# A two-layer decoder trunk on one core: routing pieces and low parts in strict turns on VectorE, scores one head ahead, the table's first tile asked for earlier

## Chip, cores and metric

One core of one Trainium2 chip runs the whole program in one launch. The metric is the device time of one execution in microseconds; lower is better. Engines are called by the profile's names: PE (TensorE, matrix multiplication), DVE (VectorE), ACT (ScalarE), POOL (GpSimd) and SP (the engine whose queue issues most DMAs).

## What is computed

A decoder trunk of two layers on 256 tokens of width 1024, float32: a recurrent block, then a stick-breaking attention block. Each is followed by the same product-key expert layer, which is where the change lies:

```python
q = (xt @ w_q).reshape(T, PEER_HEADS, 2, PEER_HALF)
s = jnp.einsum('thpd,hpnd->thpn', q, sub_keys)
sv, si = lax.top_k(s, PEER_TOPK)
cand = sv[:, :, 0, :, None] + sv[:, :, 1, None, :]
cv, ci = lax.top_k(cand.reshape(T, PEER_HEADS, PEER_TOPK * PEER_TOPK), PEER_TOPK)
i1 = jnp.take_along_axis(si[:, :, 0], ci // PEER_TOPK, axis=-1)
i2 = jnp.take_along_axis(si[:, :, 1], ci % PEER_TOPK, axis=-1)
eidx = (i1 * PEER_NKEYS + i2).reshape(T, PEER_HEADS * PEER_TOPK)
gates = jax.nn.softmax(cv, axis=-1).reshape(T, PEER_HEADS * PEER_TOPK)
...
act = jax.nn.gelu(jnp.einsum('cd,ckd->ck', xc, u_tab[ic]))
return jnp.einsum('ck,ckd->cd', gc * act, v_tab[ic])
```

There are 8 heads, 128 keys per half, 16 picks per head, and 128 x 128 = 16384 experts with a row each in the tables `u` and `v`.

## The kernel before

**The up stage.** For 224 of the 256 tokens the kernel does not gather expert rows. It multiplies the whole table `u` with the tokens in 128 tiles (`e` = 0 to 127), 128 experts each, applies gelu, multiplies by a gate that is zero for experts not picked, and then multiplies with the 128 tiles of `v` (the v stage, tile name `acc`). The other 32 tokens take their rows by gathered DMAs (`fetches`, `fetch_row`; tiles `got`, `rows`, `sums`).

**Halves.** A float32 product is made of three matmuls. `split` makes, of a raw tile, a rounded high part on ACT (`wH`, the copy in `split`) and the rest, the low part, on DVE (`wL`, line 136). A tile of 128 x 1024 takes 24 matmuls in `mm3`, lines 165 to 167; of each three, line 167's needs `wL`, so the third matmul of a tile already waits for the low part. `fetch` asks for the raw tile on SP, from a pool of three buffers `raws`, and splits it into a pool of three pairs `halves`. A raw buffer is free once ACT and DVE have read it.

**Routing.** `route` is a generator, one per head. Its first step multiplies the tokens with the two `w_q` tiles of the head, copies the result (`qT`, ACT) and multiplies it with the keys into scores `ps_s`. Each later step is a piece of DVE work: four max pieces (16 largest of 128 keys, with indices, lines 497 to 501), two candidate pieces (lines 506 to 522), one that splits the index (527 to 540), one that makes a one-hot `hot` (543), one that multiplies it (551), and one that sums it to `picks`, `places` and `shares` (556 to 564). Heads 0 and 1 have their scores before the loop. From `e` = 4 on each tile of the up stage draws two steps from the generators, one head after the other. When they are used up, the tile number is kept as `begun`, which comes out as 47.

**What follows routing.** `scatter` writes a head's gates for 128 of the tokens into a table `G` in DRAM, by indirect DMAs on POOL; the other 96 tokens' gates are made by `hots` (DVE), eight matmuls and a product in `bank_of_gates`, in 24 groups spread over the tiles from `begun` to 124. From `e` = 52 on, every fourth tile (every second from 116) makes one step of `fetches`, and draws four scatters. In the v stage the gates in `G` come back in tiles `gt` of four experts' tiles each; `gates(0)` asks for the first after the up stage's loop, and line 792 multiplies with it.

**Order.** A scheduler places each engine's instructions. `issue_after(i)` holds what is traced in its block behind the instruction `i` if it is on the same engine; pieces are held behind the last low part traced so far, `self.lows[-1]`. Low parts are not held behind pieces. `load` holds its DMA behind the last raw tile's.

Of the kernel before, what the change touches and what calls it, by code (L numbers as in the profile page):

```python
# [8 lines left out]
F32 = mybir.dt.float32  # L9
# [10 lines left out]
P = 128  # L20
# [4 lines left out]
NK = 128  # L25
# [31 lines left out]
class Trunk:  # L57


    def __init__(self, ctx, tc, a):  # L60
# [11 lines left out]
        self.n = 0  # L72
        self.lows = []

        c = self.const
# [58 lines left out]
    def split(self, raw, hi, lo):  # L134
        self.copied = self.nc.scalar.copy(out=hi, in_=raw)  # L135
        self.lows.append(self.nc.vector.tensor_tensor(out=lo, in0=raw, in1=hi.bitcast(F32), op=ALU.subtract))  # L136
        return hi, lo

# [332 lines left out]
    def route(self, l, hd, pool, xs, r):  # L471
# [21 lines left out]
        for t in range(2):  # L493
            for p in range(2):
                yield
                s, s2 = S[:, t, p], tl([P, NK], F32, "s2")
                V.max(out=sv[:, t, p, :8], in_=s)
                V.match_replace(out=s2, in_to_replace=sv[:, t, p, :8], in_values=s, imm_value=LOWEST)  # L498
                V.max(out=sv[:, t, p, 8:], in_=s2)
                V.max_index(out=si[:, t, p, :8], in_max=sv[:, t, p, :8], in_values=s)  # L500
                V.max_index(out=si[:, t, p, 8:], in_max=sv[:, t, p, 8:], in_values=s2)
        yield
# [13 lines left out]
        for t in range(2):  # L516
            s = cand[:, t]
            V.max(out=cv[:, t, :8], in_=s)
            V.match_replace(out=cand2, in_to_replace=cv[:, t, :8], in_values=s, imm_value=LOWEST)
            V.max(out=cv[:, t, 8:], in_=cand2)  # L520
            V.max_index(out=ci[:, t * K:t * K + 8], in_max=cv[:, t, :8], in_values=s)
            V.max_index(out=ci[:, t * K + 8:(t + 1) * K], in_max=cv[:, t, 8:], in_values=cand2)
            if t == 0:
                yield
# [3 lines left out]
        if r is not None:  # L528
# [10 lines left out]
        V.tensor_tensor(out=ab[:, :, 1], in0=col, in1=tail, op=ALU.subtract)  # L539
        V.tensor_tensor(out=ab[:, :, 1], in0=ab[:, :, 1], in1=b8, op=ALU.add)  # L540
        yield
        hot = tl([P, 4 * K, K], BF16, "hot")
        V.tensor_tensor(out=hot, in0=self.iota.unsqueeze(1).to_broadcast([P, 4 * K, K]),
                        in1=ab.rearrange("p k x -> p (k x)").unsqueeze(2).to_broadcast([P, 4 * K, K]),
# [3 lines left out]
        with self.tc.issue_after(self.copied.ins):  # L548
            nc.scalar.activation(gt, gt, AF.Exp)
        h4 = hot.rearrange("p (t k x) a -> p t k (x a)", t=2, x=2)  # L550
        V.tensor_tensor(out=h4, in0=h4,
                        in1=sif.rearrange("p t x a -> p t (x a)").unsqueeze(2).to_broadcast([P, 2, K, 2 * K]),
# [10 lines left out]
        V.reciprocal(gs, gs)  # L563
        V.tensor_tensor(out=self.shares[:, :, ks], in0=gt, in1=gs.to_broadcast([P, 2, K]), op=ALU.mult)
        if hd < HEADS // 2:
            for _ in self.scatter(l, hd):
                pass
        if hd % (HEADS // 2) == HEADS // 2 - 1:
            self.name_rows(hd // (HEADS // 2))
        yield  # L570
# [116 lines left out]
    def peer(self, l):  # L687
# [3 lines left out]
        with ExitStack() as ph:  # L691
            ph.enter_context(self.early_pool)
            early = self.early
            with ExitStack() as up:
                pool = up.enter_context(tc.tile_pool(name="up", bufs=1, reuse_waits="tile"))
# [37 lines left out]
                heads += [self.route(l, hd, rt, xs, None) for hd in range(NX, HEADS)]  # L733
                pieces = (hd for hd in heads for _ in hd)
                made, done, begun = [], 0, None
                writes = (i for hd in range(HEADS // 2, HEADS) for i in self.scatter(l, hd))
                rows = self.fetches(l)
                for e in range(NK):
                    if begun is None and e >= 4:
                        for _ in range(2):  # L740
                            with tc.issue_after(self.lows[-1].ins):
                                if next(pieces, None) is None:
                                    begun = begun or e
# [7 lines left out]

                    if begun and e >= 52 and (e % 4 == 0 if e < 116 else e % 2 == 0):
                        with tc.issue_after(self.lows[-1].ins):
                            next(rows)
                        with tc.issue_after(self.row.ins):
                            for _ in range(4):
# [14 lines left out]
                    if done:  # L771
                        V.tensor_tensor(out=A[:, e, split:], in0=g, in1=A[:, e, split:], op=ALU.mult)
                assert done == NQ and next(writes, None) is None
            acc = [self.ps_acc.tile([P, 2, T], F32, tag=f"acc{i}", name=self.uid("acc")) for i in range(4)]
            proj_pool = side.enter_context(tc.tile_pool(name="proj", bufs=1, reuse_waits="tile"))
            late = ph.enter_context(tc.tile_pool(name="late", bufs=3, reuse_waits="tile"))

            def gates(e):
                pool = late if e else early
                gt = pool.tile([P, NB, TS], F32, tag="gt", name=self.uid("gt"))  # L780
                self.load(gt, self.G[l].rearrange("(p e t) one -> p e (t one)", p=NK, t=TS)[:, e:e + NB])
                return gt

            ahead, tail = gates(0), []
            self.sums = late.tile([P, D], F32, tag="sums", name=self.uid("sums"), bufs=1)
# [170 lines left out]
```

## Time and profile before

| | us |
|---|---|
| median of 3 runs | 1962.94 (1960.91 to 1966.56) |
| the profiled execution | 1962.31 |
| its span, first to last instruction | 1960.6 |
| PE busy | 1857.8 (95%) |
| DVE busy | 1524.5 (78%) |
| ACT busy | 1007.3 (51%) |
| POOL busy | 740.6 (38%) |

The mean granted PE clock is 0.982. A row of the timeline gives start and length in us, engine, line, operation, the tiles it writes and reads, and in brackets the idle time of the engine just before it and what ended it. A row of the waits gives who waited for whom, the total in us, how often, and the longest. Rows of `DMA` in the chain give the start, and the time from issue to landing as far as it lies on the chain. Line numbers are those of the kernel before; in the changed kernel they stand 1 to 20 lines further down.

### The profile page before, as it was taken

The page shows a single profiled execution, that of the slowest core. Times are in us where ns is not written, and L with a number is a line of the kernel's source. Part 1 is how long each engine was busy: PE and PEld are TensorE (multiplying, and loading weights), DVE is VectorE, ACT ScalarE, POOL GpSimd, SP SyncE. Part 2 cuts the span into 40 slices and gives each one's busy share as a digit, 9 for nine tenths or more (in the row PEclk, how much of TensorE's full clock was granted, in tenths as well). Part 3 has the DMA queues.
Part 4 walks back from the last instruction along what each step waited for, and adds up shares of the span by engine and source line. Part 5 has one row for each costly group of instructions (what it writes and reads, how often), then busy time and mean ns, then how long its engine had stood idle before and what let it go on. Part 6 is the DMA issues. An engine that isn't in the chain of part 4 may idle for free.

```text
span 1960.6 us, 40513 instructions
## 1 busy us (share of the span) xinstructions
PE 1857.8 (95%) x15716; PEld 1815.1 (93%) x15716; DVE 1524.5 (78%) x3255; ACT 1007.3 (51%) x1768; POOL 740.6 (38%) x517
## 2 busy tenths in 40 slices
PE   7898889999989999999999988889999999999998
PEld 6898889999989999998887988889999999999997
DVE  6888887878877877776755787877888877777766
ACT  6764444444435454445655644445444445454446
POOL 3318771777522112110200167744877221112102
PEclk9999999999999999999999999999999999999999
DMA  8756666788878888885681566657888788888863
GB/s 278 218 175 163 150 158 185 224 218 224 227 250 296 296 285 284 290 275 177 212 266 60 164 156 165 151 168 203 228 226 222 241 292 280 290 288 282 290 223 106
DMA packets 193394, 435.73 MB, mean 222 GB/s; under 512 B 51568, under 2 KB 87536, under 8 KB 193200
## 3 DMA queue, kind: packets, MB, share of 16 engines
q1 hardware_dynamic: 137104, 365.02, 57.4%
q0 software_dynamic: 56096, 68.12, 15.3%
q8 instruction: 123, 2.02, 0.4%
q14 instruction: 71, 0.58, 0.1%
HBM read 414.25 MB, written 17.96 MB: 220 GB/s over the span
## 4 chain that ended last, share of the span: by engine, by line
PE 70%; DVE 18%; DMA 4%; ACT 4%; issue 3%; SPq 0%; POOL 0%; DVEq 0%; ACTq 0%
PE acc L167 10%; PE acc L166 10%; PE acc L165 10%; DVE wL L136 6%; PE lin L167 6%; PE lin L165 6%; PE lin L166 6%; PE u L167 4%; PE u L165 4%; PE u L166 4%; ACT wH L135 2%; PE gates L673 2%; DMA raw<-v 2%; DMA gt<-G 1%; DVE s L498 1%
## 5 line engine op out<-in xcount | busy, mean ns | idle before, releaser
L136 DVE TENSOR_TENSOR wL<-raw,wH 128x1024 fp32r<-128x1024 f32 x620 | 758.1, 1224 | 323.2 <-ACT wH L135 305.0
L135 ACT CAST wH<-raw 128x1024 fp32r<-128x1024 f32 x620 | 649.5, 1049 | 658.1 <-PE acc L166 198.6
L165 PE MATMUL acc<-aH,wH 128*128 128x224 f32 x2048 | 565.7, 276 | 7.7 <-ACT wH L135 6.2
L167 PE MATMUL acc<-aH,wL 128*128 128x224 f32 x2048 | 567.5, 277 | 1.4 <-DVE wL L136 1.4
L166 PE MATMUL acc<-aL,wH 128*128 128x224 f32 x2048 | 564.0, 275 | 0.6 <-DVE aL L136 0.3
L578 POOL DMA_INDIRECT G<-shares,places x256 | 473.7, 1850 | 138.4 <-issue 80.7
L165 PEld LDWEIGHTS acc<-aH,wH 128*128 128x128 f32 x2048 | 395.8, 193 | 8.4 <-ACT wH L135 6.6
L167 PEld LDWEIGHTS acc<-aH,wL 128*128 128x128 f32 x2048 | 395.8, 193 | 1.8 <-DVE wL L136 1.8
L166 PEld LDWEIGHTS acc<-aL,wH 128*128 128x128 f32 x2048 | 395.8, 193 | 1.3 <-DVE aL L136 0.8
L603 POOL DMA_INDIRECT got<-v,named x64 | 90.0, 1407 | 418.1 <-DVE act L792 405.3
L603 POOL DMA_INDIRECT got<-rows,named x64 | 92.0, 1438 | 240.0 <-DVE got L620 160.0
L221 POOL TENSOR_TENSOR tot<-tot,sq 128x256 f32<-128x256 f32 x36 | 30.8, 855 | 264.5 <-ACT sq L219 263.3
L135 ACT CAST aH<-act 128x224 fp32r<-128x224 f32 x256 | 95.4, 375 | 14.1 <-DVE act L792 14.1
L136 DVE TENSOR_TENSOR aL<-act,aH 128x224 fp32r<-128x224 f32 x256 | 97.8, 383 | 0.9 <-ACT aH L135 0.9
L678 ACT COPY act<-gates 128x308 f32<-128x308 f32 (+23 forms) x48 | 14.0, 292 | 140.2 <-DVE act L677 131.6
L792 DVE TENSOR_TENSOR act<-act,gt 128x128 f32<-128x128 f32 x256 | 72.4, 283 | 11.3 <-DMA gt<-G 11.3
L659 DVE SCALAR_TENSOR_TENSOR first<-ints,which,gate 128x256 fp32r<-128x256 f32 x192 | 80.6, 477 | 0.0
L625 DVE SCALAR_TENSOR_TENSOR sums<-got,heat,sums 128x1024 f32<-128x1024 f32 x62 | 79.2, 1277 | 0.0
L620 DVE SCALAR_TENSOR_TENSOR got<-got,xrow 128x1024 f32<-128x1024 f32 x64 | 77.9, 1217 | 0.0
L167 PE MATMUL lin<-x0H,wL 128*128 128x224 f32 (+1 forms) x156 | 45.6, 292 | 25.8 <-DVE wL L136 25.8
L167 PEld LDWEIGHTS lin<-x0H,wL 128*128 128x128 f32 x156 | 30.3, 194 | 29.6 <-DVE wL L136 29.6
L167 PE MATMUL u<-x0H,wL 128*128 128x224 f32 x128 | 37.4, 292 | 19.2 <-DVE wL L136 19.1
(907 smaller groups left out, 5213.6 us busy)
## 6 DMA issues: line engine op xcount, KB each, us to landing
raw<-u SPq DMA_DIRECT2D x256, 512.0 KB
raw<-v SPq DMA_DIRECT2D x256, 512.0 KB
G<-zero SPq DMA_DIRECT2D x32, 512.0 KB
raw<-w_q SPq DMA_DIRECT2D x32, 512.0 KB
gt<-G SPq DMA_DIRECT2D x64, 256.0 KB
raw<-w_in SPq DMA_DIRECT2D x16, 512.0 KB
raw<-w_gate SPq DMA_DIRECT2D x16, 512.0 KB
raw<-w_out SPq DMA_DIRECT2D x8, 512.0 KB
```

The costliest lines, as they stand in the source:

```text
L135: self.copied = self.nc.scalar.copy(out=hi, in_=raw)
L136: self.lows.append(self.nc.vector.tensor_tensor(out=lo, in0=raw, in1=hi.bitcast(F32), op=ALU.subtract))
L165: mm(out, lhsT=sH, rhs=mH, start=start, stop=False, skip_group_check=True)
L166: mm(out, lhsT=sH, rhs=mL, start=False, stop=False, skip_group_check=True)
L167: self.product = mm(out, lhsT=sL, rhs=mH, start=False, stop=stop, skip_group_check=True)
L578: i = nc.gpsimd.indirect_dma_start(out=self.G[l][:, :], out_offset=bass.IndirectOffsetOnAxis(ap=self.places[:, k:k + 1], axis=0), in_=self ...
L603: self.row = self.nc.gpsimd.indirect_dma_start(out=got[:, :], out_offset=None, in_=table, in_offset=bass.IndirectOffsetOnAxis(ap=self.name ...
L620: V.scalar_tensor_tensor(out=row, in0=row, scalar=1.0, in1=self.xrow, op0=ALU.mult, op1=ALU.mult, accum_out=heat[:, i:i + 1])
L625: V.scalar_tensor_tensor(out=self.sums, in0=row, scalar=heat[:, i:i + 1], in1=self.sums, op0=ALU.mult, op1=ALU.add)
L659: V.scalar_tensor_tensor(out=first[:, j], in0=self.ints.unsqueeze(1).to_broadcast([P, 2, NK]), scalar=self.which[:, 0, t:t + 1], in1=self. ...
L673: nc.tensor.matmul(ps[:, j], lhsT=second[:, j], rhs=first[:, j, x], start=j == 0 and x == 0, stop=x == 1, skip_group_check=True)
L792: V.tensor_tensor(out=A[:, e, :TS], in0=A[:, e, :TS], in1=gt[:, e % NB], op=ALU.mult)
```

## The change

Three things change in each of the two expert layers.

1. `route` keeps the last DVE instruction of each piece as `self.mark`, and the next low part that `split` makes is held behind it. The tiles from `e` = 4 draw one step (even `e`) or two (odd `e`) instead of two. A head's first step, with the scores, is no longer a step of its own: it is made when the fourth max piece of the head before is reached. So 80 steps are drawn instead of 86, and `begun` comes out as 57.
2. The steps of `fetches` at `e` = 52 and 56 no longer wait for `begun`. The second `name_rows`, which makes the row numbers of heads 4 to 7, moves from the last piece of head 7 to `e` = 72.
3. `gates(0)` moves from behind the up stage's loop to the end of its tile 123.

```diff
     def split(self, raw, hi, lo):
         self.copied = self.nc.scalar.copy(out=hi, in_=raw)
         self.lows.append(self.nc.vector.tensor_tensor(out=lo, in0=raw, in1=hi.bitcast(F32), op=ALU.subtract))
+        if self.mark is not None:
+            self.after(self.lows[-1], self.mark)
+            self.mark = None
         return hi, lo
...
-                V.max_index(out=si[:, t, p, 8:], in_max=sv[:, t, p, 8:], in_values=s2)
+                self.mark = V.max_index(out=si[:, t, p, 8:], in_max=sv[:, t, p, 8:], in_values=s2)
...
-        if hd % (HEADS // 2) == HEADS // 2 - 1:
-            self.name_rows(hd // (HEADS // 2))
+        if hd == HEADS // 2 - 1:
+            self.name_rows(0)
...
-                pieces = (hd for hd in heads for _ in hd)
-                made, done, begun = [], 0, None
+
+                def in_turn():
+
+                    for i, hd in enumerate(heads):
+                        for n, _ in enumerate(hd):
+                            if n == 3 and NX <= i + 1 < HEADS:
+                                next(heads[i + 1])
+                            yield
+                pieces = in_turn()
+                made, done, begun, ahead = [], 0, None, None
...
                     if begun is None and e >= 4:
-                        for _ in range(2):
+                        for _ in range(1 + e % 2):
                             with tc.issue_after(self.lows[-1].ins):
-                                if next(pieces, None) is None:
+                                if next(pieces, pieces) is pieces:
                                     begun = begun or e
...
-                    if begun and e >= 52 and (e % 4 == 0 if e < 116 else e % 2 == 0):
+                    if e >= 52 and (e % 4 == 0 if e < 116 else e % 2 == 0):
                         with tc.issue_after(self.lows[-1].ins):
                             next(rows)
+                        if e == 72:
+                            with tc.issue_after(self.lows[-1].ins):
+                                self.name_rows(1)
...
-                assert done == NQ and next(writes, None) is None
+                    if e == NK - 5:
+                        assert next(writes, None) is None
+                        ahead = gates(0)
+                assert done == NQ
...
-            ahead, tail = gates(0), []
+            tail = []
```

The same `self.mark =` stands before the last DVE instruction of every other piece of `route`. `gates` itself is moved ahead of the stage, unchanged.

On DVE, in routing of layer 0 (`wL` are low parts; `sv`, `si` and `s` are one head's values, indices and masked scores). Before, the two low parts are followed by the head's max pieces, and the next low part stands only after 42 routing instructions:

```order
L136 TENSOR_TENSOR wL_2347<-raw_2344,wH_2346 128x1024
L136 TENSOR_TENSOR wL_2398<-raw_2395,wH_2397 128x1024
L497 MAX sv_2291<-ps_s_2220 128x8
L498 MATCH_REPLACE s_371_2293<-sv_2291,ps_s_2220 128x128
L500 MAX_INDEX si_2292<-sv_2291,ps_s_2220 128x8
L499 MAX sv_2291<-s_371_2293 128x8
L497 MAX sv_2291<-ps_s_2220 128x8
L501 MAX_INDEX si_2292<-sv_2291,s_371_2293 128x8
```

In the changed kernel, at the same head:

```order
L137 TENSOR_TENSOR wL_2398<-raw_2395,wH_2397 128x1024
L501 MAX sv_2196<-ps_s_2125 128x8
L502 MATCH_REPLACE s_388_2427<-sv_2196,ps_s_2125 128x128
L504 MAX_INDEX si_2197<-sv_2196,ps_s_2125 128x8
L503 MAX sv_2196<-s_388_2427 128x8
L505 MAX_INDEX si_2197<-sv_2196,s_388_2427 128x8
L137 TENSOR_TENSOR wL_2437<-raw_2434,wH_2436 128x1024
L501 MAX sv_2196<-ps_s_2125 128x8
```

A low part now stands behind each piece or two, and the five instructions of a single piece follow each other with nothing of another piece between them.

On SP, at the end of layer 0's up stage (`raw<-u` and `raw<-v` are table tiles, `gt<-G` the gate tiles), before:

```order
L158 DMA raw_7523<-u 128x1024
L158 DMA raw_7561<-u 128x1024
L148 DMA gt_7607<-G_145 128x512
L158 DMA raw_7617<-v 128x1024
L158 DMA raw_7655<-v 128x1024
```

and in the changed kernel:

```order
L162 DMA raw_7359<-u 128x1024
L152 DMA gt_7404<-G_145 128x512
L162 DMA raw_7406<-u 128x1024
L162 DMA raw_7451<-u 128x1024
L162 DMA raw_7498<-u 128x1024
L162 DMA raw_7536<-u 128x1024
L162 DMA raw_7590<-v 128x1024
```

The first gate tile moves ahead of four loads of `u`. The second keeps its place, behind the sixth load of `v`.

More of the change, by code (lines that the diff above doesn't have):

```diff
@@ L136, in split @@
         self.lows.append(self.nc.vector.tensor_tensor(out=lo, in0=raw, in1=hi.bitcast(F32), op=ALU.subtract))
+        if self.mark is not None:
+            self.after(self.lows[-1], self.mark)
+            self.mark = None
         return hi, lo
@@ L521, in route @@
             V.max_index(out=ci[:, t * K:t * K + 8], in_max=cv[:, t, :8], in_values=s)
-            V.max_index(out=ci[:, t * K + 8:(t + 1) * K], in_max=cv[:, t, 8:], in_values=cand2)
+            self.mark = V.max_index(out=ci[:, t * K + 8:(t + 1) * K], in_max=cv[:, t, 8:], in_values=cand2)
             if t == 0:
@@ L539, in route @@
         V.tensor_tensor(out=ab[:, :, 1], in0=col, in1=tail, op=ALU.subtract)
-        V.tensor_tensor(out=ab[:, :, 1], in0=ab[:, :, 1], in1=b8, op=ALU.add)
+        self.mark = V.tensor_tensor(out=ab[:, :, 1], in0=ab[:, :, 1], in1=b8, op=ALU.add)
         yield
         hot = tl([P, 4 * K, K], BF16, "hot")
-        V.tensor_tensor(out=hot, in0=self.iota.unsqueeze(1).to_broadcast([P, 4 * K, K]),
+        self.mark = V.tensor_tensor(out=hot, in0=self.iota.unsqueeze(1).to_broadcast([P, 4 * K, K]),
                         in1=ab.rearrange("p k x -> p (k x)").unsqueeze(2).to_broadcast([P, 4 * K, K]),
@@ L550, in route @@
         h4 = hot.rearrange("p (t k x) a -> p t k (x a)", t=2, x=2)
-        V.tensor_tensor(out=h4, in0=h4,
+        self.mark = V.tensor_tensor(out=h4, in0=h4,
                         in1=sif.rearrange("p t x a -> p t (x a)").unsqueeze(2).to_broadcast([P, 2, K, 2 * K]),
@@ L563, in route @@
         V.reciprocal(gs, gs)
-        V.tensor_tensor(out=self.shares[:, :, ks], in0=gt, in1=gs.to_broadcast([P, 2, K]), op=ALU.mult)
+        self.mark = V.tensor_tensor(out=self.shares[:, :, ks], in0=gt, in1=gs.to_broadcast([P, 2, K]), op=ALU.mult)
         if hd < HEADS // 2:
@@ L693, in peer, with gates @@
             early = self.early
+            def gates(e):
+                pool = late if e else early
+                gt = pool.tile([P, NB, TS], F32, tag="gt", name=self.uid("gt"))
+                self.load(gt, self.G[l].rearrange("(p e t) one -> p e (t one)", p=NK, t=TS)[:, e:e + NB])
+                return gt
             with ExitStack() as up:
@@ L776, in peer @@
             late = ph.enter_context(tc.tile_pool(name="late", bufs=3, reuse_waits="tile"))
[L778 to L782, printed above, removed]
-            ahead, tail = gates(0), []
+            tail = []
             self.sums = late.tile([P, D], F32, tag="sums", name=self.uid("sums"), bufs=1)
```

## The prediction

> **What bounds the kernel now.** I read the page first: engine shares, and the chain of work that ended last.
>
> ```profile
> PE 1857.8 (95%) x15716; PEld 1815.1 (93%) x15716; DVE 1524.5 (78%) x3255; ACT 1007.3 (51%) x1768; POOL 740.6 (38%) x517
> PE 70%; DVE 18%; DMA 4%; ACT 4%; issue 3%; SPq 0%; POOL 0%; DVEq 0%; ACTq 0%
> ```
>
> TensorE (PE) is the bound, but VectorE (DVE) carries 18% of the chain. To see where, I asked for busy time by stretch: layer 0 and layer 1 from the first matmul of tile e=4 to that of tile e=47, where routing ends, and then a stretch of the same loop without routing.
>
> ```profile
> 131.08:325.10 194.02, 169.28 (x1377) 164.68 (x1375) 162.00 (x590) 93.83 (x134) 128.05 (x78) 0.96 0.63 160
> 1125.66:1320.88 195.22, 169.12 (x1377) 164.20 (x1375) 162.24 (x590) 93.83 (x134) 129.70 (x78) 0.96 0.63 159
> 340.00:560.00 220.00, 219.85 (x1969) 219.67 (x1969) 180.22 (x324) 104.77 (x246) 142.79 (x80) 1.00 0.81 224
> ```
>
> The columns are length, then busy us and instructions of PE, weight loads, DVE, ACT, POOL, then granted clock, DMA share, GB/s. Without routing PE is busy all the time. With routing it is idle for 24.7 us of 194 and its clock averages 0.96. What PE waits for in layer 0's stretch:
>
> ```profile
> PE lin L167 <- DVE wL L136: 12.7, 10, 2.8
> PE u L167 <- DVE wL L136: 8.5, 8, 2.6
> PE ps_s L489 <- ACT qT L487: 3.1, 6, 0.5
> ```
>
> 21.2 of the 24.7 us is a late low part (wL). The DVE timeline of one head says why, and PE's shows the effect:
>
> ```profile
> 224.64 1.23 DVE L136 TENSOR_TENSOR wL<-raw,wH 128x1024 fp32r<-128x1024 f32 x1 [0.99 <-ACT wH L135]
> 225.78 0.29 DVE L497 MAX8 sv<-ps_s 128x8 f32<-128x128 f32 x1
> 226.10 0.09 DVE L498 MATCH_VALUE_LOAD s<-sv,ps_s 128x8 f32 x1
> 226.18 0.28 DVE L498 MATCH_REPLACE8 s<-sv,ps_s 128x128 f32<-128x128 f32 x1
> 226.38 0.08 DVE L500 MATCH_VALUE_LOAD si<-sv,ps_s 128x8 f32 x1
> ...
> 235.06 1.22 DVE L136 TENSOR_TENSOR wL<-raw,wH 128x1024 fp32r<-128x1024 f32 x1
> 236.20 1.22 DVE L543 TENSOR_TENSOR hot<-iota,ab 128x1024 bf16<-128x1024 bf16 x1
> ```
> ```profile
> 236.34 0.55 PE L167 MATMUL lin<-x0H,wL 128*128 128x224 f32 x1 [2.78 <-DVE wL L136]
> ```
>
> From 225.78 to 235.06, 9.28 us, DVE runs seven routing pieces of one head with no low part between them. PE uses a tile up in under 3 us and only three pairs of halves exist, so it stops.
>
> The clock falls after such stops:
>
> ```profile
> 131.00:165.00 34.00, 28.28 (x238) 26.81 (x236) 33.02 (x126) 18.62 (x26) 18.62 (x11) 1.00 0.56 146
> 235.00:243.00 8.00, 6.66 (x32) 6.67 (x33) 7.82 (x13) 4.23 (x7) 7.08 (x4) 0.57 0.67 133
> ```
>
> Up to 165 us, where DVE does two pieces and a low part per tile, PE stops often but shortly and keeps clock 1.00; right after the 2.78 us stop it gets 0.57. The Trainium skill ("TensorE: Matmul & The Clock Gate", Part 1) says that the clock halves after at least one idle window of some 3.4 us. No routing stop is that long, so here the trace, not the page, decides; by the page the half clock would not come from these stops and would stay after the change (last of the rivals).
>
> **How much of the stretch is loss.** PE's pace where nothing stops it:
>
> ```profile
> 131.08 0.27 PE L165 MATMUL lin<-x0H,wH 128*128 128x224 f32 x1
> 133.76 0.27 PE L165 MATMUL lin<-x0H,wH 128*128 128x224 f32 x1
> 165.67 0.29 PE L165 MATMUL lin<-x0H,wH 128*128 128x256 f32 x1
> 168.48 0.28 PE L165 MATMUL lin<-x0H,wH 128*128 128x256 f32 x1
> 171.28 0.61 PE L489 MATMUL ps_s<-keys,qT 128*128 128x128 f32 x4
> 171.64 0.35 PE L165 MATMUL u<-x0H,wH 128*128 128x224 f32 x1
> 172.73 0.71 PE L489 MATMUL ps_s<-keys,qT 128*128 128x128 f32 x4 [0.52 <-ACT qT L487]
> 173.20 0.35 PE L165 MATMUL u<-x1H,wH 128*128 128x224 f32 x1
> ```
>
> A u tile takes 2.68 us, a w_q tile 2.81, a head's scores 0.36 + 0.47 = 0.83. The stretch holds 43 u tiles (e=4 to 46), 12 w_q tiles, 6 heads' scores and the turn (0.62): 115.2 + 33.7 + 5.0 + 0.6 = 154.6 us. So the loss is 194.0 - 154.6 = 39.4 us in layer 0 and 195.2 - 154.6 = 40.6 in layer 1: the waits of 24.7, some 8 from the clock (4% of 194), the rest restarts.
>
> **Part 1, strict turns at 1.5 pieces a tile, scores one head ahead.** It removes no work. Each low part now stands behind the piece before it, and 80 pieces at one and two per tile end routing at e=57, not 47. By the order of the instructions the longest run of pieces between two low parts falls from 9.28 us to two pieces. What these cost shows in head 0:
>
> ```profile
> 128.19 1.21 DVE L136 TENSOR_TENSOR wL<-raw,wH 128x1024 fp32r<-128x1024 f32 x1
> 129.32 0.29 DVE L497 MAX8 sv<-ps_s 128x8 f32<-128x128 f32 x1
> 132.10 1.20 DVE L136 TENSOR_TENSOR wL<-raw,wH 128x1024 fp32r<-128x1024 f32 x1
> 133.23 0.18 DVE L506 CAST sif<-si 128x64 bf16<-128x64 uint32 x1
> 136.08 1.21 DVE L136 TENSOR_TENSOR wL<-raw,wH 128x1024 fp32r<-128x1024 f32 x1
> ```
>
> A low part takes 1.13 us of DVE's time (128.19 to 129.32), two max pieces 2.78 (129.32 to 132.10), the two candidate pieces 2.85.
>
> DVE's total for e=4 to 56: 162.0 busy now, plus 10 more low parts (11.3), plus two row products that now fall inside (e=52 and 56, 1.14 each, as a full-width low part: 2.3), plus dependence. A dependent start costs 0.32 us (225.78 to 226.10) and an independent one 0.20 (226.18 to 226.38); some four a head lose their cover, 0.5 x 8 = 4. Sum 179.6 us. PE's floor for the same tiles: 154.6 + 10 x 2.68 = 181.4, and the qT wait stays (its place on PE is unchanged), some 4 us with restarts: 185.5. So DVE is at 97% of PE: it fits, without room.
>
> What stays lost. Lower bound: the 4 us of the qT wait. Upper bound: DVE still sits idle for its ACT half as it does now, 28.6 us:
>
> ```profile
> L136 DVE TENSOR_TENSOR wL<-raw,wH 128x1024 fp32r<-128x1024 f32 x56 | 67.9, 1220 | 28.6 <-ACT wH L135 25.6 <-issue 2.7
> ```
>
> Then DVE ends at 179.6 + 28.6 = 208.2, which is 27 us over 181.4. I take 12: 4 of the qT wait; about 1 in heads 0 and 1, where DVE has 20 pieces (a head's are (162.0 - 55 x 1.13) / 8 + 0.5 = 13.0 us) and 15.3 low parts (17.3) against PE's 13.3 tiles, two w_q tiles and scores (42.1); 3 in the last head, which has no w_q tiles (DVE 13.0 + 6.7 x 1.13 + 2.3 of rows = 22.8, PE 6.7 x 2.68 = 17.9, and low parts made ahead for part of it); and 4 for the five middle heads, where PE has 25 us of work and DVE 22.8 but two pieces in a row plus a low part (3.9 us) exceed a tile (2.68). It lies nearer the lower end because ACT's wait is mostly PE's and raw's lateness, and comes with the clump. No half clock: stops like those before 165 us keep 1.00. Gain: 39.4 - 12 = 27.4 and 40.6 - 12 = 28.6, together 56.0.
>
> The scores one head ahead cost nothing: the same 24 matmuls a tile at another place, keys loaded earlier on the sync queue, and MAX8 finds its scores ready. The Exp on ACT moves behind the next qT copy; its input is by then a piece old.
>
> **Part 2, what the ten tiles cost later.** 24 gate groups are spread over 68 tiles instead of 78, 15% more of them per tile; eight fewer gelu products give a little back. PE hides them while DVE, busy for 82% of the stretch without routing (180.22 of 220), has room; in the last twelve tiles, with a row product every second tile instead of every fourth, it has the least. I take 1 us a layer lost, between 0 (all hidden) and 3 (one stop of the size of 577.15's, quoted below). The second half's names, 3 small DVE instructions and 4 DMAs on POOL, move to e=72; their first reader is the row fetch at e=108, so nothing waits. POOL's scatters of heads 0 to 3 start later by a third; it is busy for 128.05 of 194 us and has the room.
>
> **Part 3, the first gate tile asked for at e=123.** On the sync queue the load passes four raw loads.
>
> ```profile
> 549.81 0.44 SPq L148 DMA_DIRECT2D gt<-G  x1
> 555.53 0.29 DVE L792 TENSOR_TENSOR act<-act,gt 128x128 f32<-128x128 f32 x1 [1.50 <-DMA gt<-G]
> 575.44 0.29 DVE L792 TENSOR_TENSOR act<-act,gt 128x128 f32<-128x128 f32 x1 [4.57 <-DMA gt<-G]
> 577.15 0.44 PE L165 MATMUL acc<-aH,wH 128*128 128x224 f32 x1 [3.52 <-ACT wH L135]
> 523.14 1.77 POOL L578 DMA_INDIRECT G<-shares,places  x1 [0.30 <-issue]
> ```
>
> Issued some 8 us earlier it lands before its reader, and DVE's 1.50 us wait goes; I take 1.5 a layer (bounds 0 and 1.5). It needs the last scatter, which runs at 523, long before: the sync queue is not blocked, and the four raws behind it are delayed by one 256 KB load. The larger stop, 3.52 us on PE, is the second gate tile's; its place behind six v loads and ACT's order (aH of e=4 before wH of the fourth v tile) are unchanged, so it stays, with its half clock.
>
> **Sum.** 56.0 - 2.0 + 3.0 = 57.0 us, against the profiled execution's 1962.3 (span 1960.6); the median of the runs is 1962.9, so I leave it there: 1905.
>
> **Rivals.** *PE's floor is reached*: only the qT wait stays, 4 instead of 12 a layer, 1889. For it: DVE total below PE's; against: 97%. *DVE stays the bound*: loss 20 to 27 a layer, 1921 to 1935; for it the upper bound above and the bursts of 3.9 us. *Slower*: the turn closes a loop. A low part must wait for the piece, its raw buffer is freed only then, and the next raw is cast only when landed:
>
> ```profile
> 215.28 0.33 SPq L158 DMA_DIRECT2D raw<-u  x1
> 218.71 1.05 ACT L135 CAST wH<-raw 128x1024 fp32r<-128x1024 f32 x1 [2.01 <-DMA raw<-u]
> 292.86 5.86 DMA raw<-u
> ```
>
> Landing 3.4 to 5.9, cast 1.05, low part 1.23, two pieces 2.8: 8.5 to 10.9 us for three tiles, up to 3.6 a tile; low parts now are 3.9 apart in head 0 (128.19, 132.10, 136.08). The present time for e=4 to 56 is 194.0 + 10 x 2.68 + two gate groups (0.85 each) = 222.5; without w_q tiles, scores, turn, gates and qT waits (45) that is 3.35 a tile. At 3.9 throughout, 53 x 0.55 = 29 us more a layer, 2020; it decides from 3.35 on. Against it: two pieces come only every second tile, and most landings are near 3.4. *No change*: DVE's order does not set PE's stops; the wait rows speak against it. *The clock stays low*, as the page has it: 8 us a layer less gain, 1921.
>
> **Chances.** Forecast (loss 8 to 18 a layer, 1897 to 1917) 0.60; floor (1886 to 1897) 0.11; DVE-bound (1917 to 1940) 0.17; clock stays 0.03; no change 0.03; slower 0.06. The range 1888 to 1932 leaves out slower, no change, the floor's edge and the worst of DVE-bound. Within 0.3%, 6 us, a measurement of this kernel cannot tell from no change: faster 0.91, same 0.03, slower 0.06.
>
> **What would show it.** In the changed profile, e=4 to 57 should take some 193 us (222.5 now) with PE idle under 10 and clock 1.00; the wL waits should fall from 21.2 us to a few, none over 1.5; DVE busy near 180 in it. The wait of L792's counterpart on the first gt should be gone, the second's 3.5 us stop still there. Wrong: wL waits spread over every tile, or clock under 1.00 in routing.

## The result, and the profile after

| | before | changed |
|---|---|---|
| median of 4 runs, us | 1964.61 (1960.91 to 1966.56) | 1899.89 (1895.76 to 1905.97) |
| profiled execution, us | 1962.31 | 1898.7 |
| its span, us | 1960.6 | 1897.0 |
| mean granted PE clock | 0.982 | 0.991 |

The ratio is 0.9675, with a 95% interval of 0.9644 to 0.9707: 64.7 us faster. The forecast was 1905.

Lines moved: 136 is now 137 (low part), 165 to 167 are 169 to 171 (matmuls), 487 and 489 are 491 and 493 (`qT`, scores), 497 is 501 (first maximum), 792 is 810 (gate product). The engine shares and the chain of the changed kernel's page:

```profile
PE 1834.7 (97%) x15716; PEld 1799.2 (95%) x15716; DVE 1524.5 (80%) x3237; ACT 1006.7 (53%) x1750; POOL 737.0 (39%) x517
PE 78%; DVE 11%; ACT 4%; DMA 3%; issue 3%; POOL 0%; SPq 0%; DVEq 0%; ACTq 0%
```

DVE's busy time is the same to the last digit, 1524.5 us. What fell is its part in the chain, from 18% to 11%, and PE's busy time by 23 us, which the two routing stretches below account for (198.1 to 186.2 us and 197.8 to 186.1): the matmuls are as many, and fewer of them run at half clock or are drawn out over a wait.

To see where the 63.6 us of span came from, I cut both executions at the same tiles, by the start of the gelu of tiles e=4, e=57 and e=127. First before, both layers from e=4 to e=57 and both from e=57 to e=127 (columns as in the prediction):

```profile
134.80:357.60 222.80, 198.06 (x1634) 193.46 (x1633) 181.97 (x612) 108.36 (x167) 135.97 (x82) 0.96 0.63 167
1129.40:1353.30 223.90, 197.80 (x1632) 192.88 (x1632) 182.12 (x611) 108.16 (x166) 137.54 (x82) 0.96 0.64 166
357.60:567.50 209.90, 208.94 (x1867) 208.39 (x1866) 173.60 (x313) 99.54 (x237) 137.35 (x79) 1.00 0.82 229
1353.30:1564.70 211.40, 209.37 (x1866) 208.54 (x1866) 173.76 (x313) 99.59 (x237) 137.51 (x79) 1.00 0.82 227
```

Then the changed kernel, e=4 to 57 in both layers, and e=57 to 127 in both:

```profile
139.80:329.80 190.00, 186.21 (x1638) 184.74 (x1637) 175.56 (x597) 107.90 (x158) 132.46 (x79) 1.00 0.76 196
1101.30:1291.80 190.50, 186.09 (x1635) 184.43 (x1634) 175.79 (x597) 107.80 (x158) 131.84 (x79) 1.00 0.75 195
329.80:539.20 209.40, 208.50 (x1863) 207.94 (x1862) 180.20 (x327) 99.67 (x237) 133.25 (x82) 1.00 0.83 228
1291.80:1501.30 209.50, 208.78 (x1866) 208.23 (x1865) 180.10 (x327) 99.80 (x236) 137.47 (x82) 1.00 0.80 228
```

| stretch | layer 0 | layer 1 |
|---|---|---|
| e=4 to 57 | 222.8 to 190.0: -32.8 | 223.9 to 190.5: -33.4 |
| e=57 to 127 | -0.5 | -1.9 |

These make -68.6. The rest of the two layers moved by 0.2 at most, and the stretch ahead of layer 0's table, which the change does not touch, took 5.0 us more in this execution (that stretch lay between 125.5 and 130.7 us over all profiles here). So the two routing stretches are the whole gain, as forecast, and between e=57 and 127 DVE takes on some 6.5 us more work (173.6 to 180.2) and PE still waits for almost nothing (208.5 busy of 209.4).

The cut at the gelu is not quite even. In the changed kernel the gelu of e=57 starts 6.1 us after PE's first matmul of that tile, because ACT stood 3.29 us waiting for a raw tile just before; in the kernel before, and at e=4 in both, it starts 3.7 to 3.8 us after. Cut at PE's first matmuls, as the prediction cuts, e=4 to 57 is this, before and then changed:

```profile
131.08:353.76 222.68, 197.94 (x1633) 193.34 (x1631) 181.90 (x624) 108.14 (x163) 132.44 (x81) 0.96 0.63 165
1125.66:1349.54 223.88, 197.78 (x1633) 192.86 (x1631) 182.15 (x624) 108.03 (x163) 134.09 (x81) 0.96 0.64 164
```
```profile
136.10:323.67 187.57, 183.78 (x1616) 182.31 (x1615) 174.66 (x601) 107.48 (x154) 127.24 (x76) 1.00 0.75 191
1097.58:1285.98 188.40, 184.00 (x1616) 182.33 (x1615) 174.91 (x601) 107.40 (x154) 126.93 (x76) 1.00 0.74 190
```

So the routing stretches are 35.1 and 35.5 us shorter, of which 1.7 us each are two gate groups that PE did ahead of e=57 before and does behind it now. From e=57 to the end of the v stage the changed kernel takes 1.7 and 0.3 us more, those groups included.

What PE still waits for between e=4 and 57 of layer 0, and DVE's low parts there (busy, mean ns, then idle time before them and what ended it):

```profile
PE ps_s L493 <- ACT qT L491: 2.2, 4, 0.6
PE u L171 <- DVE wL L137: 0.6, 2, 0.3
PE ps_s L493 <- ACT wH L136: 0.5, 1, 0.5
PE ps_s L493 <- issue: 0.5, 1, 0.5
```
```profile
L137 DVE TENSOR_TENSOR wL<-raw,wH 128x1024 fp32r<-128x1024 f32 x65 | 78.5, 1216 | 9.7 <-ACT wH L136 9.2 <-issue 0.3 <-ACT act L791 0.2
```

The late low part has gone as PE's wait: 21.2 us before, 0.6 now, none over 0.3. The six stops at the scores stay. DVE's idle time ahead of its low parts fell from 28.6 us (25.6 of it for the ACT half) to 9.7 (9.2).

### The profile page after: what moved, and what is told of

Its sections match the earlier page's. It is cut to its first block, busy times and chain, and to the rows that moved or that the text cites. A ratio compares the mean times of both kernels' runs of the same rounds, so it can differ in the third digit from the quotient of the medians.

```text
span 1897.0 us, 40427 instructions
## 1 busy us (share of the span) xinstructions
PE 1834.7 (97%) x15716; PEld 1799.2 (95%) x15716; DVE 1524.5 (80%) x3237; ACT 1006.7 (53%) x1750; POOL 737.0 (39%) x517
## 4 chain that ended last, share of the span: by engine, by line
PE 78%; DVE 11%; ACT 4%; DMA 3%; issue 3%; POOL 0%; SPq 0%; DVEq 0%; ACTq 0%
PE acc L171 12%; PE acc L170 12%; PE acc L169 12%; PE lin L169 7%; PE lin L170 6%; PE lin L171 6%; DVE wL L137 5%; PE u L171 5%; PE u L169 5%; PE u L170 5%; ACT wH L136 2%; PE gates L677 2%; DMA raw<-u 1%; PE ps_s L493 1%; DMA gt<-G 1%
## 5 line engine op out<-in xcount | busy, mean ns | idle before, releaser
L582 POOL DMA_INDIRECT G<-shares,places x256 | 465.9, 1820 | 145.5 <-issue 79.3
L607 POOL DMA_INDIRECT got<-v,named x64 | 98.5, 1538 | 410.8 <-DVE act L810 410.8
L607 POOL DMA_INDIRECT got<-rows,named x64 | 87.3, 1363 | 211.7 <-DVE got L624 132.2
L682 ACT COPY act<-gates 128x272 f32<-128x272 f32 (+23 forms) x48 | 13.3, 276 | 144.3 <-DVE act L681 142.0
L677 PE MATMUL gates<-first,second 128*128 128x128 f32 x384 | 48.6, 269 | 0.0
L677 PEld LDWEIGHTS gates<-first,second 128*128 128x128 f32 x384 | 46.7, 192 | 0.0
L169 PE MATMUL lin<-x0H,wH 128*128 128x224 f32 (+1 forms) x156 | 44.8, 287 | 0.6 <-ACT act L791 0.6
```

The lines of the kernel that those rows point to most:

```text
L169: mm(out, lhsT=sH, rhs=mH, start=start, stop=False, skip_group_check=True)
L582: i = nc.gpsimd.indirect_dma_start(out=self.G[l][:, :], out_offset=bass.IndirectOffsetOnAxis(ap=self.places[:, k:k + 1], axis=0), in_=self ...
L607: self.row = self.nc.gpsimd.indirect_dma_start(out=got[:, :], out_offset=None, in_=table, in_offset=bass.IndirectOffsetOnAxis(ap=self.name ...
L677: nc.tensor.matmul(ps[:, j], lhsT=second[:, j], rhs=first[:, j, x], start=j == 0 and x == 0, stop=x == 1, skip_group_check=True)
```

## The experiments

All kernels are timed against the same kernel before (medians 1962.7 to 1964.4 in the three sets). Unless said otherwise the edit is made to the changed kernel.

### Are the strict turns what helps?

**no_turns.** The dependence of the low part on the piece before it is dropped:

```diff
         if self.mark is not None:
-            self.after(self.lows[-1], self.mark)
             self.mark = None
```

> The changed kernel without the dependence that holds a low part behind the piece before it; pace (one and two pieces a tile) and scores one head ahead stay. Theory 'strict turns are what counts': the clumps come back, routing loses some 39 us a layer again, 1960 us. Theory 'the scores asked ahead and the slower pace are what counts; the scheduler then alternates by itself': the order on VectorE hardly differs from the changed kernel's (longest run of routing instructions between two low parts 14 in both, 43 in the kernel before), and the time stays at 1900 us within 4.

Measured: 1899.78 us (1897.83 to 1901.84), ratio 0.9675 (0.9647 to 0.9704), which is the changed kernel's. The same stretch in its trace, layer 0:

```profile
137.90:327.10 189.20, 185.41 (x1631) 183.94 (x1629) 175.23 (x597) 107.77 (x158) 136.06 (x79) 1.00 0.73 196
```

The order of the instructions says why: before, up to 43 routing instructions stood between two low parts; without the turns but with the scores ahead, at most 14 do, as many as with the turns. With the scores ahead the scheduler makes the turns by itself, and holding it to them buys nothing.

### The three parts of the edit by themselves

The first part of the change is three edits: turns, pace (one and two steps instead of two), and scores one head ahead. Five more kernels fill in most of the table.

**two_a_tile**, the pace of before:

```diff
-                        for _ in range(1 + e % 2):
+                        for _ in range(2):
```

> The changed kernel with two pieces at every tile, so that routing ends at e=44 instead of 57; strict turns and scores ahead stay. Theory 'VectorE's load per tile counts': 52 low parts x 1.13 + 8 heads x 13 = 163 us of VectorE's work for e=4 to 43 stand against 40 x 2.68 + 33.7 + 5 + 4 = 150 us of TensorE's, so some 13 us more are lost a layer, many stops of about 1 us at every tile and clock 1.00: 1926 us. Theory 'only the clump counts': 1900 us.

**scores_in_place**, a head's scores a step of its own again, at the head's own beginning:

```diff
                         for n, _ in enumerate(hd):
-                            if n == 3 and NX <= i + 1 < HEADS:
-                                next(heads[i + 1])
                             yield
```

> The changed kernel with a head's scores as a step of its own just ahead of its first max piece, as in the kernel before; strict turns and one and two pieces a tile stay (routing ends at e=61). Theory 'asking ahead counts': VectorE waits at each head for two w_q tiles, the qT copy and the scores, 6 us a head, of which the lead in low parts hides half: some 15 us more a layer, 1930 us. Theory 'turns and pace suffice': low parts of the w_q tiles fill the wait, 1903 us.

**only_ahead**, the edits of no_turns and two_a_tile together, so that of the three the scores ahead alone are left:

> The changed kernel with two pieces a tile and without strict turns: of part 1 only the scores one head ahead are left. Theory 'asking ahead breaks the clump': the longest run of routing instructions between low parts is 14, and the time is that of two pieces a tile with strict turns, 1926 us. Theory 'strict turns break it': clumps of 9 us, half clock after them, 1955 us.

**only_turns**, the kernel before with the marks and the dependence alone (the rest of its routing as before):

```diff
         self.lows.append(...)
+        if self.mark is not None:
+            self.after(self.lows[-1], self.mark)
+            self.mark = None
```

> The kernel before with strict turns alone: two pieces a tile, scores as a step of their own, first gate tile asked for after the stage. Theory 'VectorE's load per tile counts once the clump is broken': 55 low parts x 1.13 + 8 x 13 = 166 us of VectorE's work for e=4 to 46 against 155 + 4 of TensorE's, plus waits for scores: loss of 15 to 25 us a layer instead of 39, 1925 to 1940 us. Theory 'the forecast's slower rival, the closed loop': every tile 3.9 us, 1990 us or more.

**only_pace**, the edits of no_turns and scores_in_place together, so that the pace alone is left:

> The changed kernel without strict turns and with the scores in place: of part 1 only the pace of one and two pieces a tile is left. Runs of up to 29 routing instructions (some 6 us) stand between low parts. Theory 'the clump counts': stops of 1 to 2 us with half clock after some, 1915 to 1930 us. Theory 'pace alone suffices': 1903 us.

| turns | pace 1.5 | scores ahead | kernel | us | ratio to before |
|---|---|---|---|---|---|
| no | no | no | before | 1963 to 1965 | 1 |
| yes | no | no | only_turns | 1994.65 | 1.0158 (1.0138 to 1.0178) |
| no | yes | no | only_pace | 1923.56 | 0.9788 (0.9767 to 0.981) |
| yes | yes | no | scores_in_place | 1961.04 | 0.9982 (0.9968 to 0.9996) |
| no | no | yes | only_ahead | 1914.74 | 0.9755 (0.9723 to 0.9787) |
| yes | no | yes | two_a_tile | 1914.43 | 0.9750 (0.9722 to 0.9778) |
| no | yes | yes | no_turns | 1899.78 | 0.9675 (0.9647 to 0.9704) |
| yes | yes | yes | changed | 1899.89 | 0.9675 (0.9644 to 0.9707) |

(only_turns lacks the second and third part of the change as well; the others have them. The traces put them at 1.3 us together, see "Parts 2 and 3" below.)

Read in pairs: the turns do nothing with the scores ahead (rows 5 and 6, 7 and 8) and cost 31 to 37 us without (1 and 2, 3 and 4). The pace is worth some 15 us with the scores ahead and 34 to 40 without. The scores ahead are worth 24 us at the new pace without turns, 49 at the old one, and 61 to 80 with turns. Most of my numbers here missed: two_a_tile lies between 1926 and 1900, only_ahead 11 us below 1926, and scores_in_place lost all of the gain, where 1930 was the most that I had allowed. Of only_turns' values the worst, 1990 or more, came true, though not by the loop that it was given for. The kernel only_pace lies in its range, 1915 to 1930. The parts are not additive: pace and scores ahead each take away much of the same loss, and either alone brings most of the gain, 40 and 49 of 65 us. In only_pace the clump is still there (29 to 31 routing instructions between two low parts, 6.9 to 8.1 us), but PE waits only 7.1 us for low parts and the clock stays 1.00 (e=4 to 57 of layer 0; in this kernel, no_turns and only_ahead the lines 171 and 493 are 170 and 492):

```profile
139.10:340.30 201.20, 188.92 (x1626) 184.66 (x1625) 170.29 (x584) 107.52 (x155) 139.30 (x79) 1.00 0.71 183
PE lin L170 <- DVE wL L137: 4.3, 7, 1.5
PE u L170 <- DVE wL L137: 2.8, 7, 0.6
```

**Why the turns are harmful without the scores ahead.** DVE's waits in only_turns, e=4 to 57 of layer 0, and PE's:

```profile
DVE sv L501 <- PE ps_s L493: 37.0, 6, 8.0
PE lin L171 <- DVE wL L137: 15.7, 15, 2.4
PE u L171 <- DVE wL L137: 15.5, 15, 2.4
```

The timeline of one such wait, DVE's rows first and then the scores on PE and the next late low part:

```profile
225.07 2.47 DVE L137 TENSOR_TENSOR wL<-raw,wH 128x1024 fp32r<-128x1024 f32 x2
235.56 0.30 DVE L501 MAX8 sv<-ps_s 128x8 f32<-128x128 f32 x1 [8.03 <-PE ps_s L493]
```
```profile
234.81 0.71 PE L493 MATMUL ps_s<-keys,qT 128*128 128x128 f32 x4 [0.51 <-ACT qT L491]
238.30 0.56 PE L171 MATMUL lin<-x0H,wL 128*128 128x224 f32 x1 [2.44 <-DVE wL L137]
```

DVE has made all the low parts that the three pairs of halves hold. Next in its order comes the head's first maximum, whose scores stand on PE behind those very tiles. So DVE sits idle for 8.03 us while PE works off the stock. ACT meanwhile starts the high parts of three further tiles (at 228.82, 231.08 and 233.45), but by the strict turn their low parts stand behind the piece. When the scores come at 234.81, PE has no low part left, DVE starts its pieces at 235.56, and at 238.30 PE has waited 2.44 us. DVE waits like this at each of the six heads, and PE stops for 1.5 to 2.4 us after each. In scores_in_place the same wait takes 32.1 us for the six:

```profile
DVE sv L501 <- PE ps_s L493: 32.1, 6, 8.3
```

Before has no such row: its scheduler, free to move low parts, ran them ahead and let the pieces gather into a clump behind the scores. How late the scores were, the traces show at the clump of the prediction, at 225.78. PE's last scores of that head and, in the changed kernel, the same head's scores and first maximum:

```profile
224.93 0.71 PE L489 MATMUL ps_s<-keys,qT 128*128 128x128 f32 x4 [0.52 <-ACT qT L487]
```
```profile
217.34 0.71 PE L493 MATMUL ps_s<-keys,qT 128*128 128x128 f32 x4 [0.52 <-ACT wH L136]
225.88 0.29 DVE L501 MAX8 sv<-ps_s 128x8 f32<-128x128 f32 x1
```

Before, the first maximum starts 0.14 us after the scores end (225.64), and so it does at every head after the first two, in both layers; in the changed kernel it starts 5.8 to 8.0 us after. The clump was the answer to late scores. Asking for the scores earlier takes away the cause; forbidding the clump takes away only the answer.

**Why the pace matters.** At two steps a tile one head takes five tiles. By the prediction's own prices DVE then has 13.0 + 7 x 1.13 = 20.9 us in a head with its w_q tiles (five low parts of u, two of w_q), and PE 5 x 2.68 + 2 x 2.81 + 0.83 = 19.9: by these prices DVE is the bound. At 1.5 steps the same prices give 22.8 against 24.3. In only_ahead, e=4 to 57 of layer 0, and what PE waits for there:

```profile
138.20:340.80 202.60, 189.89 (x1641) 186.04 (x1641) 183.14 (x614) 109.63 (x171) 131.93 (x79) 1.00 0.70 184
```
```profile
PE ps_s L492 <- ACT qT L490: 5.3, 7, 1.0
PE lin L170 <- DVE wL L137: 5.1, 6, 1.0
PE u L170 <- DVE wL L137: 2.1, 4, 0.6
```

The trace bears this out in part: 7.2 us of PE's waits are for low parts, but 5.3 are for `qT`, and DVE itself waits 14.0 us for high parts. The stops are short and the clock stays 1.00; the stretch takes 12.6 us more than in the changed kernel, and 3.0 of that comes back after e=57 (206.4 against 209.4), where three gate groups less are left to do.

### How much room has DVE?

**one_more_index** repeats one instruction in each max piece:

```diff
                 V.max_index(out=si[:, t, p, :8], in_max=sv[:, t, p, :8], in_values=s)
+                V.max_index(out=si[:, t, p, :8], in_max=sv[:, t, p, :8], in_values=s)
```

> The changed kernel with the first FIND_INDEX8 of each max piece made twice: 32 more in a layer, 0.08 + 0.20 us each by the timeline, 9 us of DVE. DVE's busy time between e=4 and 57 is 175.6 us of 190 in the changed kernel; this puts it at 184.5, 97% of the stretch, which is what the prediction had reckoned for the changed kernel itself. Theory A, the prediction's: at 97% the pieces cost PE some 8 us a layer beyond the qT stops, so the time is 1910 to 1918 and u <- wL waits appear. Theory B: low parts run far enough ahead that DVE fits until it is full, and the prediction's 8 us were wrong in kind and not only by its 4 us too much DVE: 1900 to 1903, with waits under 2 us.

Measured: 1905.11 us (1904.10 to 1909.68), ratio 0.9712 (0.9694 to 0.973). The two stretches, and PE's two longest waits in layer 1's:

```profile
139.40:331.30 191.90, 185.43 (x1623) 183.38 (x1622) 180.88 (x654) 107.90 (x158) 145.87 (x76) 1.00 0.70 190
1107.10:1300.60 193.50, 185.55 (x1623) 183.37 (x1622) 181.25 (x655) 107.78 (x157) 145.36 (x76) 1.00 0.70 188
```
```profile
PE ps_s L493 <- ACT qT L491: 5.0, 6, 2.3
PE u L171 <- DVE wL L137: 1.6, 2, 1.3
```

Between the theories, and my price of the edit was off: it added 5.4 us of DVE a layer, not 9, so DVE came to 94% of the stretch and not to the 97% that I wanted to test. At 94% these stretches are 1.9 and 3.0 us longer than the changed kernel's; cut at PE's first matmuls they are 191.2 and 192.7 us against 187.6 and 188.4, so 3.6 and 4.3 longer. By the medians it is 5.2 us for both layers. What the price is at 97% stays open.

### What of the loss is left

**scores_a_tile_late** asks for w_q and `qT` at the neighbour's second piece and for the scores at its fourth, with a tile of u between them:

```diff
+        qTs = []
...
             nc.scalar.copy(out=qT, in_=pss[p])
+            qTs.append(qT)
+        if hd > 1:
+            yield
+        for p, qT in enumerate(qTs):
             for t in range(2):
...
-                            if n == 3 and NX <= i + 1 < HEADS:
+                            if n in (1, 3) and NX <= i + 1 < HEADS:
```

> The changed kernel with a head's first step cut in two: w_q and the qT copies at its neighbour's second piece, the scores' matmuls at the fourth. So at least one tile of u lies on PE between the qT copy and the matmul that reads it. In the changed kernel PE still stops six times a layer for qT, 0.8 us each with the restart, 4.8 of the 6.6 to 7.2 us that the stretch e=4 to 57 loses to its floor. Theory A, the qT stop is most of the loss that is left: the stretch falls to 185 to 186 us (190.0 and 190.5 now), no ps_s <- qT wait is left, and the time is 1889 to 1892. Theory B, the stops only hide that DVE is the bound (the prediction's 97%): the u <- wL waits grow by what the qT waits lose, and the time stays within 3 us of 1899.8.

Measured: 1889.34 us (1882.93 to 1891.97), ratio 0.9633 (0.9616 to 0.965). The stretches, and all that PE waits for in layer 0's:

```profile
136.00:321.60 185.60, 185.03 (x1637) 184.50 (x1637) 175.19 (x596) 107.76 (x158) 137.97 (x79) 1.00 0.76 200
1091.90:1277.10 185.20, 184.73 (x1637) 184.34 (x1636) 175.24 (x597) 107.55 (x157) 137.72 (x79) 1.00 0.76 200
```
```profile
PE lin L171 <- DVE wL L137: 0.3, 1, 0.3
PE u L171 <- DVE wL L137: 0.3, 1, 0.3
```

Theory A, to the number: the stops at the scores were a true loss of 4.4 and 5.3 us, and DVE, at 94% of the shorter stretch, does not take it back.

### The gate tiles

**gate_tile_late** puts `gates(0)` behind the loop again:

```diff
-                    if e == NK - 5:
-                        assert next(writes, None) is None
-                        ahead = gates(0)
...
-            tail = []
+            ahead, tail = gates(0), []
```

> The changed kernel with the first gate tile asked for after the up stage, as before: part 3 undone. VectorE's wait of 1.5 us a layer on that tile comes back. Theory 'TensorE feels it': 2 to 3 us more, 1902.5 us. Theory 'hidden': the wait shows on VectorE, TensorE's stops before the first v tile are the same, 1900 us.

Measured: 1899.88 us (1898.05 to 1903.67), ratio 0.9678 (0.9656 to 0.97): no difference that these runs can tell. In its trace DVE waits 0.76 us for the first gate tile in layer 0, where it was 1.50 before, and not at all in layer 1; in the changed kernel it waits for it in neither.

**second_gate_early** asks for the second gate tile at tile 123 too, and for each later one four tiles sooner:

```diff
-                pool = late if e else early
-                gt = pool.tile([P, NB, TS], F32, tag="gt", name=self.uid("gt"))
+                pool = late if e > NB else early
+                gt = pool.tile([P, NB, TS], F32, tag="gt", name=self.uid("gt"), bufs=None if e > NB else 2)
...
-                        ahead = gates(0)
+                        ahead = [gates(0), gates(NB)]
...
-                    gt, ahead = ahead, gates(e + NB) if e + NB < NK else None
+                    gt = ahead.pop(0)
+                    if e + 2 * NB < NK:
+                        ahead.append(gates(e + 2 * NB))
```

> The changed kernel with the second gate tile too asked for at tile 123, into a second buffer of the early pool, and each later one a tile of four earlier. Theory 'the stop of 3.5 us at the fourth v tile is the second gate tile's landing, and the half clock is that stop's': stop and 6.8 us of half clock go in both layers, 2 x (3.5 + 1 + 3.4) = 16 us less, 1884 us. Rival, 'the order on ScalarE and the raw tiles bound it anyway': 1896 to 1900 us.

Measured: 1894.67 us (1890.74 to 1899.08), ratio 0.9654 (0.9633 to 0.9676): 5 us where I had 16 or nothing to 4. DVE's wait for the second gate tile and the stop on PE in the changed kernel, and what is in its place in second_gate_early:

```profile
547.14 0.29 DVE L810 TENSOR_TENSOR act<-act,gt 128x128 f32<-128x128 f32 x1 [4.55 <-DMA gt<-G]
548.84 0.37 PE L169 MATMUL acc<-aH,wH 128*128 128x224 f32 x1 [3.49 <-ACT wH L136]
```
```profile
535.04 0.37 PE L169 MATMUL acc<-aH,wH 128*128 128x224 f32 x1 [2.15 <-DVE act L793]
```

In layer 1 the stop and its half clock are gone. In layer 0 a stop of 2.15 us comes instead, for a gelu product of the first tiles, and 3.4 us of half clock with it.

**qT_and_second_gate** is scores_a_tile_late and second_gate_early in one.

> The edit of scores_a_tile_late and that of second_gate_early together. They act at different places (e=4 to 57, and the start of the v stage), so their gains should add: 1884 to 1887 if the qT stops are a true loss (8 to 10 us from them, 5 from the gate tile), 1892 to 1895 if DVE takes back what the qT stops leave.

Measured: 1879.84 us (1876.42 to 1883.09), ratio 0.958 (0.9561 to 0.9599), the fastest here, below the 1884 to 1887 expected. It is 20 us below the changed kernel, where the two alone make 10.5 + 5.2 = 15.7. The stop at 535.04 is missing in its trace, in both layers. Some 60 us into the v stage two short ones appear instead, one behind the other, with 3.4 us of half clock. Why the two edits together avoid the long one I did not test. Nor do the traces show where its gain over scores_a_tile_late lies: the two profiled executions took 1883.07 and 1882.93 us, the first near the highest of its five and the second the lowest of its five, and no stretch from e=4 on differs by more than 0.5 us.

## Why the prediction came out right, and where it did not

**The bound and the mechanism** held: PE was stopped by the clump on DVE, the half clock came from the stops, and both went. Clock 0.96 to 1.00, wL waits 21.2 to 0.6 us, PE idle 3.8 us in the stretch (forecast: under 10), and the stretch 187.6 and 188.4 us by the prediction's cut (forecast: some 193).

**The step that got the cause wrong** is "Each low part now stands behind the piece before it", with "The scores one head ahead cost nothing" as a side remark. The gain was put down to the turns. The runs show the reverse: no_turns has all of it, and the turns alone make the kernel 31 us slower. The scores ahead are what ends the clump, by themselves worth 49 us, and the pace alone is worth 40. The clump in the trace of before begins with MAX8 on `ps_s`, a tile that PE writes; I did not ask when PE had written it. The sum came out because the order that I read in the changed kernel was the true one, whatever had made it. As to the cause that was luck: by the same reasoning the turns alone would have been forecast as a gain.

**The mis-sized term** is the loss left: 12 us a layer, measured 187.6 - 181.4 = 6.2 and 188.4 - 181.4 = 7.0 over the prediction's own floor. Of its four items the qT wait was right: 4 forecast, 4.4 and 5.3 by scores_a_tile_late. The other three, 1 for heads 0 and 1, 3 for the last head and 4 for the middle ones, were 8 together; with the qT stops out some 2 us are left for all of them. I had set each burst of DVE against one tile of PE; that three pairs of halves let DVE make up over several tiles is the likely reason, not a tested one. The DVE total was also too high: 179.6 forecast, 175.6 measured, which is 162.0 + 11.3 + 2.3 without the 4 for dependence. So DVE was at 92%, not 97%.

**The pace** was priced as ten more tiles, never as a term of its own. It is worth some 15 us beside the scores ahead and 40 alone, and that it mattered could be had from the numbers that were there (20.9 against 19.9 a head).

**Parts 2 and 3.** Forecast was 1 us a layer lost and 1.5 won, net 1.0 for both layers. Measured from PE's first matmul of e=57 to the end of the v stage: 1.7 and 0.3 us more than before, with two gate groups a layer, 3.4 us in all, moved in from ahead of e=57, so 1.3 us won. The net was right, its terms were not. In gate_tile_late the same two stretches are 0.8 us longer than in the changed kernel in layer 0 and no longer in layer 1: the early gate tile is worth that and not 1.5 a layer. And with 1.3 won in all, the ten tiles' gates cost nothing that shows, where 2.0 had been taken. The errors cancelled. These are differences under 1 us between single traces, so the terms are known no better than that. The second gate tile's stop stayed, as forecast: 3.49 us.

**The rivals.** "DVE stays the bound" needed DVE's idle time ahead of low parts to stay at 28.6 us; it fell to 9.7. "PE's floor" would have needed the three small items at zero; they are 2. "The clock stays low", after the Trainium skill ("TensorE: Matmul & The Clock Gate", Part 1), needed half clock without long stops; there is none in either routing stretch. The slower rival, the closed loop over raw buffers, appears in no run here. What does make a kernel with turns slower is another loop, which I had not listed: pieces that wait for scores that stand behind the tiles whose low parts wait behind the pieces.

## To carry to other kernels

When work clumps on an engine, look at what the first instruction of the clump waited for, before forbidding the clump: the clump can be the scheduler's way round a late input, and a fixed order then turns lateness into idleness on both engines. Asking for the input one unit earlier was worth more here than any order, and the pace at which pieces are drawn should leave the side engine below the bound in each unit, here a head, and not only in the total. An edit made of several parts is priced part by part only after each was built alone: here either of two parts would have brought most of the gain alone, and the third was harmless only because of one of them.

## What the runs showed of the hardware

How short a stop brings the half clock: in the routing stretches of before, only_turns and scores_in_place PE stopped 15 times for 2.44 to 2.85 us, and each time a stretch of half clock of 3.41 or 6.83 us began within 1.4 us of the stop's end, before or after it. After single stops of 1.0 to 1.6 us it never did. Between them it was mixed: stops of 1.68, 1.71, 2.14 and 2.25 us were followed by it, others of 2.26 and 2.27 not. In the v stage of qT_and_second_gate two stops of 0.91 to 0.97 us, 1.3 us apart, were followed by 3.41 us of it in both layers. One long stop with it and one without, only_turns at 180.69 and one_more_index at 1238.56, each followed by the stretch around it (granted clock 0.70 and 1.00, third number from the end):

```profile
180.69 0.56 PE L171 MATMUL u<-x0H,wL 128*128 128x224 f32 x1 [2.44 <-DVE wL L137]
```
```profile
177.00:185.00 8.00, 5.35 (x27) 5.17 (x28) 6.84 (x29) 0.15 (x1) 4.46 (x3) 0.70 0.34 66
```
```profile
1238.56 0.38 PE L493 MATMUL ps_s<-keys,qT 128*128 128x128 f32 x1 [2.27 <-ACT qT L491]
```
```profile
1234.00:1242.00 8.00, 5.73 (x51) 5.55 (x50) 5.89 (x20) 2.56 (x5) 5.30 (x4) 1.00 0.79 203
```

The Trainium skill ("TensorE: Matmul & The Clock Gate", Part 1) puts the fall at one idle window or more, of some 3.4 us. The lengths of half clock here, 3.41 and twice that, agree with such windows; the stops named above were all shorter than one.

The traces say more. In each of the thirteen, all starts and ends of half clock in the two table stages (130 to 620 and 1095 to 1600 us) lie on one grid of 3.413 us, to within 4 ns. I summed PE's idle time, by the modelled ends of its matmuls, in each window of that grid that was at full clock. After all 39 windows with 1.84 us or more of it half clock followed, after none of the 3654 with less than 1.25, and in between after 4 of 28. So these traces fit a rule by which the idle time within one window counts, with a limit near half of it, and a window need not be wholly idle. It sorts the mixed cases: the stop of 2.25 us lay within one window, the one of 2.27 was shared by two, 1.83 us of it in the first, and the two short stops of qT_and_second_gate shared one. No run was made to test the rule.
